# An im2col kernel bound by its DMA engines: eight consecutive channels per partition, and half of the input loaded beside the first stores

## The chip, the cores and the metric

One core of a Trainium2 chip. The metric is the device time of the kernel in microseconds (us), as median of several runs. The profile describes one execution; its span (91.3 us before) is shorter than the timed figure (92.9 us) by 1.6 us.

## The reference

The input is 16 images of 64 channels of 32 x 32 float32 numbers. Each channel gives nine output planes of 30 x 30: the channel shifted by (ki, kj), ki and kj from 0 to 2.

```python
for i in range(h_out):
    for j in range(w_out):
        patch = x[b, :, i:i + kernel_size, j:j + kernel_size].copy()
        cols[b, :, col_idx] = patch.ravel()
        col_idx += 1
```

No arithmetic is done. 1,024 channels of 4,096 bytes come in (4.19 MB), and 1,024 x 9 planes of 3,600 bytes go out (33.18 MB).

## The kernel before

A row is two consecutive channels, and a group is 128 rows, one for each partition. All four groups are loaded at the start. VectorE and ScalarE take turns to copy the nine shifted windows of each channel into an output tile, and SyncE stores the tile. The first group is stored one channel at a time, the others in one piece. There are two output tiles, so the third group waits until the first is stored.

```python
x_v = x.rearrange("b (cp c2) h w -> (b cp) c2 (h w)", c2=CPP)        # CPP = 2
...
for g in range(n_groups):                                            # 4 loads of 1 MB
    nc.sync.dma_start(out=in_tile, in_=x_v[row0 : row0 + P]...)
...
for g in range(n_groups):
    out_tile = out_pool.tile([P, CPP, KK, HO, WO], x.dtype)          # bufs=2
    for c2 in range(CPP):
        for kk in range(KK):
            ...
            if ncopy % 2 == 0:
                nc.scalar.copy(out=dst, in_=src)
            else:
                nc.vector.tensor_copy(out=dst, in_=src)
        if g == 0:
            nc.sync.dma_start(out=out_v[row0 : row0 + P, c2], ...)   # 32,400 bytes per partition
    if g != 0:
        nc.sync.dma_start(out=out_v[row0 : row0 + P]..., ...)        # 64,800 bytes per partition
```

Of the kernel before, what the change touches and what calls it, by code (L numbers as in the profile page):

```python
# [1 line left out]

# [4 lines left out]


def _im2col_fast(ctx, tc, x, K, out, CPP):  # L10
    nc = tc.nc
    P = nc.NUM_PARTITIONS

    B, C, H, W = x.shape
    HO = H - K + 1
    WO = W - K + 1
    KK = K * K

    ROWS = B * C // CPP
    n_groups = ROWS // P  # L20

    x_v = x.rearrange("b (cp c2) h w -> (b cp) c2 (h w)", c2=CPP)
    out_v = out.rearrange("b (cp c2 kk) n -> (b cp) c2 (kk n)", c2=CPP, kk=KK)

    in_pool = ctx.enter_context(tc.tile_pool(name="in_pool", bufs=n_groups))
    out_pool = ctx.enter_context(tc.tile_pool(name="out_pool", bufs=2))

    in_tiles = []
    for g in range(n_groups):
        row0 = g * P  # L30
        in_tile = in_pool.tile([P, CPP, H, W], x.dtype, name="in_tile")
        nc.sync.dma_start(
            out=in_tile,
            in_=x_v[row0 : row0 + P].rearrange("r c2 (h w) -> r c2 h w", h=H),
        )
        in_tiles.append(in_tile)

    for g in range(n_groups):
        row0 = g * P
        in_tile = in_tiles[g]  # L40
        out_tile = out_pool.tile([P, CPP, KK, HO, WO], x.dtype)

        ncopy = 0
        for c2 in range(CPP):
            for kk in range(KK):
                ki, kj = divmod(kk, K)
                src = in_tile[:, c2, ki : ki + HO, kj : kj + WO]
                dst = out_tile[:, c2, kk]
                if ncopy % 2 == 0:
                    nc.scalar.copy(out=dst, in_=src)  # L50
                else:
                    nc.vector.tensor_copy(out=dst, in_=src)  # L52
                ncopy += 1

            if g == 0:
                nc.sync.dma_start(
                    out=out_v[row0 : row0 + P, c2],
                    in_=out_tile[:, c2].rearrange("p kk i j -> p (kk i j)"),
                )

        if g != 0:
            nc.sync.dma_start(
                out=out_v[row0 : row0 + P].rearrange("r c2 n -> r (c2 n)"),
                in_=out_tile.rearrange("p c2 kk i j -> p (c2 kk i j)"),
            )


def _im2col_generic(ctx, tc, x, K, out):
    nc = tc.nc
    P = nc.NUM_PARTITIONS  # L70

    B, C, H, W = x.shape
    HO = H - K + 1
    WO = W - K + 1
    KK = K * K

    x_rows = x.rearrange("b c h w -> (b c) (h w)")
    out_rows = out.rearrange("b ck n -> (b ck) n").rearrange(
        "(bc kk) n -> bc (kk n)", kk=KK
    )  # L80

    n_rows = B * C
    n_groups = (n_rows + P - 1) // P

    in_pool = ctx.enter_context(tc.tile_pool(name="in_pool", bufs=min(n_groups, 4)))
    out_pool = ctx.enter_context(tc.tile_pool(name="out_pool", bufs=2))

    for g in range(n_groups):
        row0 = g * P
        nrows = min(P, n_rows - row0)  # L90

        in_tile = in_pool.tile([P, H, W], x.dtype, name="in_tile_g")
        nc.sync.dma_start(
            out=in_tile[:nrows],
            in_=x_rows[row0 : row0 + nrows].rearrange("r (h w) -> r h w", h=H),
        )

        out_tile = out_pool.tile([P, KK, HO, WO], x.dtype, name="out_tile_g")
        for kk in range(KK):
            ki, kj = divmod(kk, K)  # L100
            src = in_tile[:nrows, ki : ki + HO, kj : kj + WO]
            dst = out_tile[:nrows, kk]
            if kk % 2 == 0:
                nc.scalar.copy(out=dst, in_=src)
            else:
                nc.vector.tensor_copy(out=dst, in_=src)

        nc.sync.dma_start(
            out=out_rows[row0 : row0 + nrows],
            in_=out_tile[:nrows].rearrange("p kk i j -> p (kk i j)"),  # L110
        )


@with_exitstack
def kernel(
    ctx: ExitStack,
    tc: tile.TileContext,
    x: bass.AP,
    kernel_size: bass.AP,
    out: bass.AP,  # L120
):
    nc = tc.nc
    P = nc.NUM_PARTITIONS

    K = int(kernel_size)
    B, C, H, W = x.shape
    HO = H - K + 1
    WO = W - K + 1
    KK = K * K
    assert out.shape == (B, C * K * K, HO * WO)  # L130

    dt_size = mybir.dt.size(x.dtype)

    CPP = 0
    for cand in (2, 1):
        if C % cand:
            continue
        rows = B * C // cand
        if rows % P:
            continue  # L140
        free_bytes = cand * KK * HO * WO * dt_size
        if free_bytes >= 2**16:
            continue
        n_groups = rows // P
        sbuf_need = 2 * free_bytes + n_groups * cand * H * W * dt_size
        if sbuf_need > 190 * 1024:
            continue
        CPP = cand
        break

    if CPP:
        _im2col_fast(ctx, tc, x, K, out, CPP)
    else:
        _im2col_generic(ctx, tc, x, K, out)


# [1 line left out]
_INS = ['x', 'kernel_size']  # L158
_OUTS = [((16, 576, 900), 'float32')]
#: Inputs that are plain numbers.  # L160
_NUMBERS = {'kernel_size': 3}


# [26 lines left out]
```

## Time and profile before

| | before |
|---|---|
| time, median of three runs | 92.85 us (92.7 to 93.08) |
| span of the profile | 91.3 us |
| DMA queue's share of 16 engines' span | 95.7% |
| first load packet starts / last data packet ends | 1.75 / 89.91 us |
| VectorE, ScalarE busy | 22%, 35% |

The trace's packet records: each of the 16 DMA engines moves the data of eight partitions, one packet for each partition and DMA. These records are what the DMA rows of the views sum up, and they are this document's finest measure. They do not name the engine: what is said of single engines comes from fitting the end of one packet to the start of the next. One caution for the views in short windows: a packet is counted whole in the window in which it starts. When packets are long, a share can stand above 1.00, or at 0.00 in the next window, while the engine was simply busy. The windows below are 2 us long and are used only where packets are short.

### The profile page before, as it was taken

Reading aid. Unit: us, or ns where it says so; the run is one execution under the profiler, and the core shown is the slowest. Engines: PE = TensorE matmul, PEld = TensorE weight load, DVE = VectorE, ACT = ScalarE, POOL = GpSimd, SP = SyncE. Lnnn points to the kernel's source line nnn. Section 1 sums busy time; section 2 is a strip of 40 time slices with the busy share of each in tenths; the row PEclk is TensorE's granted clock in tenths of the full one; section 3 lists DMA queues with packets and bytes.
Section 4 is the critical chain, followed back from the end, with each engine's and each line's share of the span. In section 5 each row is a group of like instructions: output and inputs, shape, how many; then the busy total and the mean of one; then the engine's idle time right before and its main releaser. Section 6 shows DMA issues by size and latency. Waiting matters only on the chain.

```text
span 91.3 us, 141 instructions
## 1 busy us (share of the span) xinstructions
DVE 19.6 (22%) x36; ACT 32.0 (35%) x37; POOL 0.2 (0%) x4
## 2 busy tenths in 40 slices
DVE  0059997000000049600000199000000000000000
ACT  5059999991000049980000199920000000000000
POOL 0000000000000000000000000000000000000000
DMA  2899999999999999899999999999999999999960
GB/s 36 373 406 431 427 463 426 412 440 440 426 426 440 554 454 398 369 426 398 454 454 454 454 454 454 454 454 454 454 454 426 426 398 398 426 426 426 426 284 0
DMA packets 1297, 37.37 MB, mean 409 GB/s; under 512 B 145, under 2 KB 145, under 8 KB 145
## 3 DMA queue, kind: packets, MB, share of 16 engines
q1 hardware_dynamic: 1296, 37.37, 95.7%
q14 instruction: 1, 0.00, 0.0%
HBM read 4.19 MB, written 33.18 MB: 409 GB/s over the span
## 4 chain that ended last, share of the span: by engine, by line
DMA 40%; ACT 24%; ACTq 1%; issue 0%
DMA out_dram<-out_tile 34%; ACT out_tile L50 24%; DMA in_tile<-in_x_dram 5%; ACTq L185 1%; ACTq L50 0%
## 5 line engine op out<-in xcount | busy, mean ns | idle before, releaser
L50 ACT COPY out_tile<-in_tile 128x900 f32<-128x900 f32 x36 | 30.7, 938 | 27.2 <-DMA out_dram<-out_tile 23.6
L52 DVE COPY out_tile<-in_tile 128x900 f32<-128x900 f32 x36 | 19.6, 623 | 37.6 <-DMA out_dram<-out_tile 31.9
L50 ACT ACT_TABLE_LOAD x1 | 1.3, 1283 | 0.7 <-PEq L171 0.7
L171 POOL MEMSET const-bfloat16-1.0<- 128x1 bf16 x1 | 0.1, 102 | 0.0
L171 POOL MEMSET const-uint8-127<- 128x1 uint8 x1 | 0.1, 102 | 0.0
L171 POOL MEMSET const-float32-0.0<- 128x1 f32 x1 | 0.1, 99 | 0.2 <-issue 0.2
L171 POOL MEMSET const-float32-1.0<- 128x1 f32 x1 | 0.1, 99 | 0.0
## 6 DMA issues: line engine op xcount, KB each, us to landing
out_dram<-out_tile SPq DMA_DIRECT2D x3, 8100.0 KB, 30.5
out_dram<-out_tile SPq DMA_DIRECT2D x2, 4050.0 KB, 16.6
in_tile<-in_x_dram SPq DMA_DIRECT2D x4, 1024.0 KB, 7.9
```

The costliest lines, as they stand in the source:

```text
L50: nc.scalar.copy(out=dst, in_=src)
L52: nc.vector.tensor_copy(out=dst, in_=src)
L171: nc = _bacc.Bacc("TRN2", target_bir_lowering=False, num_devices=1)
L185: with _tile.TileContext(nc) as tc:
```

## The change

The intent is to start storing earlier. Every partition now owns eight consecutive channels. The input is cut into loads of one, one, two and four channels; the first three are issued at once from ScalarE's queue, and the fourth from the same queue beside the first stores. The first channel is stored in three pieces of three planes. VectorE takes three of five copies instead of every second.

```diff
-    CPP = 0
-    for cand in (2, 1):
...
+    CPP = B * C // P                                   # 8
+    x_v = x.rearrange("b (cp c2) h w -> (b cp) c2 h w", c2=CPP)
+    loads = [(0, 1), (1, 2), (2, CPP // 2), (CPP // 2, CPP)]
...
+    for i in range(len(loads) - 1):
+        load(i, nc.scalar)
+    turn = (0, 1, 0, 1, 0)
+    n = 0
+    for c in range(0, CPP, 2):
+        out_tile = out_pool.tile([P, 2, KK, HO, WO], x.dtype, name="out_tile")
+        for s in range(2):
+            for kk in range(KK):
+                plane(out_tile[:, s], c + s, kk, turn[n % len(turn)])
+                n += 1
+                if c == 0 and s == 0 and kk % K == K - 1:
+                    store(c, 1, kk + 1 - K, kk + 1, out_tile, 0)
+            if c == 0 and s == 1:
+                store(1, 1, 0, KK, out_tile, 1)
+            if c == 0 and s == 0:
+                load(len(loads) - 1, nc.scalar)
+        if c > 0:
+            store(c, 2, 0, KK, out_tile, 0)
```

More of the change, by code (lines that the diff above doesn't have):

```diff
@@ L5 @@
 import concourse.tile as tile
-from concourse import bass_utils, mybir
+from concourse import mybir
 from concourse._compat import with_exitstack
-def _im2col_fast(ctx, tc, x, K, out, CPP):
-    nc = tc.nc
-    P = nc.NUM_PARTITIONS
-    B, C, H, W = x.shape
-    HO = H - K + 1
-    WO = W - K + 1
-    KK = K * K
-    ROWS = B * C // CPP
-    n_groups = ROWS // P
-    x_v = x.rearrange("b (cp c2) h w -> (b cp) c2 (h w)", c2=CPP)
-    out_v = out.rearrange("b (cp c2 kk) n -> (b cp) c2 (kk n)", c2=CPP, kk=KK)
-    in_pool = ctx.enter_context(tc.tile_pool(name="in_pool", bufs=n_groups))
-    out_pool = ctx.enter_context(tc.tile_pool(name="out_pool", bufs=2))
-    in_tiles = []
-    for g in range(n_groups):
-        row0 = g * P
-        in_tile = in_pool.tile([P, CPP, H, W], x.dtype, name="in_tile")
-        nc.sync.dma_start(
-            out=in_tile,
-            in_=x_v[row0 : row0 + P].rearrange("r c2 (h w) -> r c2 h w", h=H),
-        )
-        in_tiles.append(in_tile)
-    for g in range(n_groups):
-        row0 = g * P
-        in_tile = in_tiles[g]
-        out_tile = out_pool.tile([P, CPP, KK, HO, WO], x.dtype)
-        ncopy = 0
-        for c2 in range(CPP):
-            for kk in range(KK):
-                ki, kj = divmod(kk, K)
-                src = in_tile[:, c2, ki : ki + HO, kj : kj + WO]
-                dst = out_tile[:, c2, kk]
-                if ncopy % 2 == 0:
-                    nc.scalar.copy(out=dst, in_=src)
-                else:
-                    nc.vector.tensor_copy(out=dst, in_=src)
-                ncopy += 1
-            if g == 0:
-                nc.sync.dma_start(
-                    out=out_v[row0 : row0 + P, c2],
-                    in_=out_tile[:, c2].rearrange("p kk i j -> p (kk i j)"),
-                )
-        if g != 0:
-            nc.sync.dma_start(
-                out=out_v[row0 : row0 + P].rearrange("r c2 n -> r (c2 n)"),
-                in_=out_tile.rearrange("p c2 kk i j -> p (c2 kk i j)"),
-            )
@@ L68, in _im2col_generic @@
-def _im2col_generic(ctx, tc, x, K, out):
-    nc = tc.nc
-    P = nc.NUM_PARTITIONS
-    B, C, H, W = x.shape
-    HO = H - K + 1
-    WO = W - K + 1
-    KK = K * K
-    x_rows = x.rearrange("b c h w -> (b c) (h w)")
-    out_rows = out.rearrange("b ck n -> (b ck) n").rearrange(
-        "(bc kk) n -> bc (kk n)", kk=KK
-    )
-    n_rows = B * C
-    n_groups = (n_rows + P - 1) // P
-    in_pool = ctx.enter_context(tc.tile_pool(name="in_pool", bufs=min(n_groups, 4)))
-    out_pool = ctx.enter_context(tc.tile_pool(name="out_pool", bufs=2))
-    for g in range(n_groups):
-        row0 = g * P
-        nrows = min(P, n_rows - row0)
-        in_tile = in_pool.tile([P, H, W], x.dtype, name="in_tile_g")
-        nc.sync.dma_start(
-            out=in_tile[:nrows],
-            in_=x_rows[row0 : row0 + nrows].rearrange("r (h w) -> r h w", h=H),
-        )
-        out_tile = out_pool.tile([P, KK, HO, WO], x.dtype, name="out_tile_g")
-        for kk in range(KK):
-            ki, kj = divmod(kk, K)
-            src = in_tile[:nrows, ki : ki + HO, kj : kj + WO]
-            dst = out_tile[:nrows, kk]
-            if kk % 2 == 0:
-                nc.scalar.copy(out=dst, in_=src)
-            else:
-                nc.vector.tensor_copy(out=dst, in_=src)
-        nc.sync.dma_start(
-            out=out_rows[row0 : row0 + nrows],
-            in_=out_tile[:nrows].rearrange("p kk i j -> p (kk i j)"),
-        )
@@ L129 @@
     KK = K * K
-    assert out.shape == (B, C * K * K, HO * WO)
-    dt_size = mybir.dt.size(x.dtype)
-    CPP = 0
-    for cand in (2, 1):
-        if C % cand:
-            continue
-        rows = B * C // cand
-        if rows % P:
-            continue
-        free_bytes = cand * KK * HO * WO * dt_size
-        if free_bytes >= 2**16:
-            continue
-        n_groups = rows // P
-        sbuf_need = 2 * free_bytes + n_groups * cand * H * W * dt_size
-        if sbuf_need > 190 * 1024:
-            continue
-        CPP = cand
-        break
@@ L151 @@
-    if CPP:
-        _im2col_fast(ctx, tc, x, K, out, CPP)
-    else:
-        _im2col_generic(ctx, tc, x, K, out)
+    assert out.shape == (B, C * KK, HO * WO)
+    CPP = B * C // P
+    assert CPP * P == B * C and C % CPP == 0 and CPP % 4 == 0
+    x_v = x.rearrange("b (cp c2) h w -> (b cp) c2 h w", c2=CPP)
+    out_v = out.rearrange("b (cp c2 kk) n -> (b cp) c2 kk n", c2=CPP, kk=KK)
+    in_pool = ctx.enter_context(tc.tile_pool(name="in_pool", bufs=1))
+    out_pool = ctx.enter_context(tc.tile_pool(name="out_pool", bufs=2))
@@ new lines, with load, plane @@
+    loads = [(0, 1), (1, 2), (2, CPP // 2), (CPP // 2, CPP)]
+    home = {}
+    def load(i, queue):
+        c0, c1 = loads[i]
+        t = in_pool.tile([P, c1 - c0, H, W], x.dtype, name=f"in_tile{i}")
+        queue.dma_start(
+            out=t.rearrange("p c h w -> p (c h w)"),
+            in_=x_v[:, c0:c1].rearrange("p c h w -> p (c h w)"),
+        )
+        for c in range(c0, c1):
+            home[c] = (t, c0)
+    def plane(dst, c, kk, engine):
+        t, base = home[c]
+        ki, kj = divmod(kk, K)
+        src = t[:, c - base, ki : ki + HO, kj : kj + WO]
+        if engine == 0:
+            nc.vector.tensor_copy(out=dst[:, kk], in_=src)
+        else:
+            nc.scalar.copy(out=dst[:, kk], in_=src)
@@ new lines, in store @@
+    def store(c, n, k0, k1, t, slot):
+        if n == 1:
+            nc.sync.dma_start(
+                out=out_v[:, c, k0:k1].rearrange("p kk n -> p (kk n)"),
+                in_=t[:, slot, k0:k1].rearrange("p kk i j -> p (kk i j)"),
+            )
+        else:
+            nc.sync.dma_start(
+                out=out_v[:, c : c + n].rearrange("p c kk n -> p (c kk n)"),
+                in_=t.rearrange("p c kk i j -> p (c kk i j)"),
+            )
+    for i in range(len(loads) - 1):
+        load(i, nc.scalar)
```

## The prediction

> **What bounds the kernel now.** I read the busy tenths in 40 slices first, because it says at once which resource has no holes.
>
> ```profile
> DVE  0059997000000049600000199000000000000000
> ACT  5059999991000049980000199920000000000000
> DMA  2899999999999999899999999999999999999960
> ```
>
> VectorE and ScalarE work in three short bursts and are empty more than half of the time; the DMA row is 8 or 9 from the second slice to the last but one. Next the totals and the queues:
>
> ```profile
> DMA packets 1297, 37.37 MB, mean 409 GB/s; under 512 B 145, under 2 KB 145, under 8 KB 145
> ## 3 DMA queue, kind: packets, MB, share of 16 engines
> q1 hardware_dynamic: 1296, 37.37, 95.7%
> ...
> HBM read 4.19 MB, written 33.18 MB: 409 GB/s over the span
> ```
>
> The 16 DMA engines are busy 95.7% of the 91.3 us span. What is left is the two ends. To find them I cut the start into windows of 0.4 us (columns: stretch, length, DVE, ACT, POOL, TensorE clock, DMA share, GB/s):
>
> ```profile
> 0.80:1.20 0.40, 0.00 (x0) 0.40 (x1) 0.00 (x0) 1.00 0.00 0
> 1.20:1.60 0.40, 0.00 (x0) 0.40 (x1) 0.00 (x0) 1.00 0.00 0
> 1.60:2.00 0.40, 0.00 (x0) 0.40 (x1) 0.00 (x0) 1.00 1.19 164
> 2.00:2.40 0.40, 0.00 (x0) 0.01 (x1) 0.00 (x0) 1.00 0.28 41
> 2.40:2.80 0.40, 0.00 (x0) 0.00 (x0) 0.00 (x0) 1.00 0.50 184
> 2.80:3.20 0.40, 0.00 (x0) 0.00 (x0) 0.00 (x0) 1.00 1.01 430
> ```
>
> From 2.8 us on the rate is the full one and stays there. The packet records of the trace, which these views sum up, give the other end: the first load packet starts at 1.64 us, the last data packet ends at 89.79 us, and the sixteen engines finish between 88.72 and 89.79. So 1.6 us lie before the DMA work, 1.5 us behind it, and 88.1 us are DMA work with no hole. Then I asked for the chain of waits in order of time and the timeline, to see whether any copy ever kept the DMA engines waiting:
>
> ```profile
> 5.61 15.29 ACT L50 COPY out_tile<-in_tile 128x900 f32<-128x900 f32 x18 [3.60 <-DMA in_tile<-in_x_dram]
> 5.61 9.77 DVE L52 COPY out_tile<-in_tile 128x900 f32<-128x900 f32 x18 [5.61 <-DMA in_tile<-in_x_dram]
> 9.96 3.72 SPq L56 DMA_DIRECT2D out_dram<-out_tile  x2
> 20.92 39.36 SPq L62 DMA_DIRECT2D out_dram<-out_tile  x3
> 33.09 7.70 ACT L50 COPY out_tile<-in_tile 128x900 f32<-128x900 f32 x9 [12.20 <-DMA out_dram<-out_tile]
> ```
>
> The first store is issued at 9.96 us, while the packets of the four loads run until 13.27 us (first of the stores: 12.20). The later stores are issued at 20.9, about 40.8 and 60.0 us, and by the packet records the work queued ahead of each lasts until some 31, 51 and 70 us. Each store is in the queue some 10 us before its turn, except the first, which has 2.2 us. The chain that ended last names ScalarE for 24% of the span, but that is the way back through the issue of a store that then stood in a queue; it is not time that a faster copy would save.
>
> **What the Trainium skill says.** "DMA: Bandwidth & Descriptors", section "Where 436 GB/s comes from", puts the ceiling of the 16 ports at 435.2 GB/s. The trace agrees: a packet of 64,800 bytes takes 2,394 ns, which is 27.07 bytes per ns and 433 GB/s on 16 engines. The same page, "Issuing engines are not separate DMA queues", says that DMAs from ScalarE and SyncE run on the same 16 engines and interleave, so that a second issuing engine only saves issue time; the kernel before uses one queue, so its trace cannot show it. The same page, "Latency and other measured facts", reports that large power-of-two row pitches in HBM slow copies (207 GB/s per direction at 512 KiB against a full 214, much less at 2 MiB and up); here no run shows it yet. "ScalarE: Activation LUTs", "What ACT_TABLE_LOAD costs", gives 1283 ns for the table load, and that page has it placed right before the first activation; the trace has exactly 1,283 ns, at 0.72 us.
>
> **The change, part by part.**
>
> Bytes: none added or removed. Still 4.19 MB in and 33.18 MB out, with the longest contiguous run of a store unchanged (two channels, 64,800 bytes).
>
> Packets: each DMA engine serves 8 partitions, one packet per partition and DMA. The trace has 309 ns for 8,192 bytes, 1,200 ns for 32,400, 2,394 ns for 64,800. The line through the last two is 0.0369 ns per byte with some 6 ns per packet. Before, one engine does 32 load packets (mean 330 ns with the slow first ones, 10.57 us), 16 of 1,200.8 ns (19.21 us), 24 of 2,394.3 ns (57.46 us), and 9 semaphore writes of 9 ns: 87.32 us. After: loads 8 x (157 + 157 + 309 + 610) ns = 9.86 us plus the same 0.67 us for the slow start, 10.53 us; stores 24 x 405 ns (three planes, 10,800 bytes) = 9.72, 8 x 1,200.8 = 9.61, 24 x 2,394.3 = 57.46; 11 semaphore writes, 0.10. Sum 87.42 us, 0.1 us more than before.
>
> Start of the copies: the first load is now 0.5 MB instead of 1 MB. Before, its packets were done on the last engine at 5.12 us and the copies began at 5.61. Half of the 8 packets' time saved, 8 x 155 ns = 1.24 us, makes this 3.88 and 4.37 us. That is 1.24 us earlier for VectorE and ScalarE, but in a stage in which the DMA engines still have loads to do, so by itself it is worth nothing.
>
> First store: it needs two VectorE and one ScalarE copies. Back to back these step by 9.77/18 = 0.54 us and 15.29/18 = 0.85 us; the last result is there at about 5.5 to 5.6 us, the issue follows within 0.1 us, and a DMA takes some 0.9 us from its issue to its first packet (0.73 to 1.64 at the start). So the first store can flow at 6.6 us. The three early loads (2.1 MB) keep the engines busy until 7.2 to 7.6 us (the second 1 MB load of before ended there). Slack 0.6 us or more, no hole. This is why the split does no harm: the half that was taken from ahead of the stores runs beside them, but it costs the same engine time there.
>
> Afterwards: stores 2 and 3 are issued near 6.6 and 7.9 us, the late load (behind four ScalarE copies) near 7.9. Work in the queues then reaches to 7.4 + 3 x 3.24 + 4.88 = 22 us. Channel 1 is stored from about 10.9 us, the next pair from about 17, when the queues hold work until 31.6. The third pair waits for its buffer until about 32 and needs 6 to 7 us of copies, while work is queued until about 51; the fourth repeats this at 51 and 70. Never closer than 11 us. The new 3:2 split of the copies between VectorE and ScalarE (11 and 7 of 18 in the first pair: 11 x 0.54 = 6.0 and 7 x 0.85 = 5.9 us, against 7.65 us for nine on ScalarE) is a real saving of 1.7 us per pair on a path that has 11 us to spare: worth nothing.
>
> The sum is +0.1 us on 92.85.
>
> **The rivals.**
>
> The loads start late. They now stand in ScalarE's queue. If the table load comes ahead of them there, the first DMA is issued 1.28 us later and all follows: 92.95 + 1.28 = 94.2. For it: in the trace before, the table load runs at 0.72 us, first thing. Against it: it bears the line of the first copy and the skill has it right before that copy, so the three issues (0.8, 0.4, 0.4 us) should precede it, and it then ends at 3.6 us, before the data is there at 4.4. One in five.
>
> Strided HBM. A partition's neighbour is now 32 KiB away on the input and 259,200 bytes on the output (before: contiguous). The input pitch is a power of two, but far below those named; the output pitch is not one. The trace speaks for the port as limit, with HBM having room. If the loads ran at half rate: the early ones would delay everything by up to 5 us, hence 95 to 98. One in twenty.
>
> Loads free beside stores. If reading and writing could go on at once on an engine, the late 2.1 MB (4.9 us) would cost less: 88 to 91. Against it: store packets alone already fill every engine. One in twenty.
>
> A smaller matter is the 1.07 us by which the engines finish apart, which goes back to their uneven start; another start could give or take 0.5 us.
>
> **Range and chances.** The main case has 92.0 to 93.5 (the 0.5 us of the uneven end either way), the late table load 94.2. Predicted 92.9, range 91.9 to 94.3. Two per cent is 1.86 us: faster needs free loads, slower needs strided HBM or a late start plus something else. 5%, 88%, 7%.
>
> **What would show it right or wrong.** Right: DMA row at 9 through the whole span, first packet near 1.6 us, copies from about 4.4 us, first store issued near 5.7 us, no window with a lower DMA share around 7 us, last packet near 90 us; the engines' share near 96%. The table load after the three issues, at about 2.3 us. Wrong: a first packet near 2.9 us (late table load); load packets of 4,096 bytes much above 157 ns or stores of 64,800 above 2,394 ns (stride); a share of the engines clearly below 95% with holes near 7 us (first store too late); or total DMA rate above 435 GB/s between 8 and 22 us (free loads).

## More of the kernel before

All packet times in the document itself count from the first instruction, as the views do. Those in the recorded prediction and expectations were counted from another record: they are 0.12 us too low for the kernel before, and 0.08 us too high for every other run.

The lines that carry the reading of before stand in the prediction. Two more are needed for comparison, the windows of 2 us around the end of the loads (columns: stretch, length, VectorE, ScalarE, GpSimd, TensorE clock, DMA share, GB/s):

```profile
8.00:10.00 2.00, 2.00 (x5) 2.00 (x4) 0.00 (x0) 1.00 0.99 418
10.00:12.00 2.00, 2.00 (x5) 2.00 (x3) 0.00 (x0) 1.00 1.03 406
```

## The result, and the profile after

The changed kernel takes 93.22 us (93.11 to 93.32, four runs) against 92.89 us (92.70 to 93.08) in the same rounds. The ratio is 1.0034, 95% interval 1.0017 to 1.0050. The forecast was 92.9 us, 91.9 to 94.3, "within 2%" at 88%. It held. The change is slower by a third of a per cent, which is small but clear of noise.

The first views to compare are the busy tenths and the queues:

```profile
DVE  0099999100000059800000199400000000000000
ACT  0599999100000059940000199400000000000000
DMA  3899899999889999999999999999999857999990
```

```profile
q1 hardware_dynamic: 1008, 33.18, 84.3%
q10 hardware_dynamic: 576, 4.19, 12.2%
```

The engines' copies moved to the left as intended, and ScalarE's bursts became shorter. The DMA row is as full as it was, and so is the sum of the two queues: 96.5% against 95.7%. The dent near the end (5 and 7) is the counting by start of the 64,800-byte packets; by the packet records the engines are busy there.

The timeline shows the schedule that came out:

```profile
0.73 1.33 ACTq L44 DMA_DIRECT2D in_tile<-in_x_dram  x3
2.10 1.28 ACT L58 ACT_TABLE_LOAD   x1 [2.10 <-issue]
...
4.49 11.92 DVE L56 COPY out_tile<-in_tile 128x900 f32<-128x900 f32 x22 [4.49 <-DMA in_tile<-in_x_dram]
4.50 0.34 ACTq L44 DMA_DIRECT2D in_tile<-in_x_dram  x1
5.34 11.07 ACT L58 COPY out_tile<-in_tile 128x900 f32<-128x900 f32 x13
5.75 5.16 SPq L62 DMA_DIRECT2D out_dram<-out_tile  x4
```

Copies start at 4.49 us and the first store is issued at 5.75 us, 4.2 us earlier than before. Two things differ from the forecast. The late load is issued at 4.50 us, although it stands behind four ScalarE copies in the source. Either the framework moved it forward, as it did in late_sp below, or the sequencer hands copies to its engine and goes on; the trace does not show which. And the first store packet starts only at 9.62 us by the packet records, 3.87 us after the issue. In that time the engines were busy but slow:

```profile
6.00:8.00 2.00, 2.00 (x5) 2.00 (x4) 0.00 (x0) 1.00 1.12 434
8.00:10.00 2.00, 2.00 (x5) 2.00 (x3) 0.00 (x0) 1.00 0.96 314
10.00:12.00 2.00, 2.00 (x4) 2.00 (x3) 0.00 (x0) 1.00 1.00 419
```

The DMA share is 0.96 and only 314 GB/s moved. That is most of the result in one line. It is not a hole: the engines count as busy, but each packet takes longer. From 7.2 to 10.4 us the 16,384-byte packets of the late load take up to 1,032 ns; later, alternating one by one with 10,800-byte store packets, nearly all take 611 ns.

The list of issues (bytes of each, median us from issue to landing) has the same wait in it. A store of 1,350 KB needs 3.2 us of the engines (8 packets of 406 ns each), yet the median of the three lands 13.2 us after its issue:

```profile
out_dram<-out_tile SPq DMA_DIRECT2D x3, 1350.0 KB, 13.2
...
in_tile<-in_x_dram ACTq DMA_DIRECT2D x1, 2048.0 KB, 11.4
```

The sums of packet time for one engine, semaphore writes left out:

| | before | predicted | after |
|---|---|---|---|
| load packets | 10.57 us | 10.53 | 11.14 |
| store packets | 76.68 us | 76.79 | 76.89 |
| sum | 87.25 us | 87.32 | 88.02 |
| engines finish | 88.85 to 89.91 | | 89.57 to 89.86 |

One engine works 0.78 us longer (the mean of the 16), and the mean engine finishes 0.38 us later; the difference is idle time, half of it at the start (0.23 us idle per engine from 1.7 to 2.5 us, against 0.43 before). In these two profiled runs the last packet even ends 0.05 us earlier, because the engines finish within 0.29 us of each other instead of 1.06 us. The timed runs put the difference at 0.33 us.

### The profile page after: what moved, and what is told of

Same layout as the page of the kernel before. It is cut to its first block, busy times and chain, and to the rows that moved or that the text cites. A ratio compares the mean times of both kernels' runs of the same rounds, so it can differ in the third digit from the quotient of the medians.

```text
span 91.3 us, 145 instructions
## 1 busy us (share of the span) xinstructions
DVE 23.4 (26%) x43; ACT 26.1 (29%) x30; POOL 0.2 (0%) x4
## 4 chain that ended last, share of the span: by engine, by line
DMA 43%; DVE 19%; DVEq 1%; issue 0%; SPq 0%
DMA out_dram<-out_tile 39%; DVE out_tile L56 19%; DMA in_tile<-in_x_dram 4%; DVEq L122 1%; DVEq L56 0%; SPq L67 0%
## 5 line engine op out<-in xcount | busy, mean ns | idle before, releaser
L58 ACT COPY out_tile<-in_tile 128x900 f32<-128x900 f32 x29 | 24.8, 939 | 30.0 <-DMA out_dram<-out_tile 28.9
L56 DVE COPY out_tile<-in_tile 128x900 f32<-128x900 f32 x43 | 23.4, 625 | 34.8 <-DMA out_dram<-out_tile 30.3
## 6 DMA issues: line engine op xcount, KB each, us to landing
out_dram<-out_tile SPq DMA_DIRECT2D x3, 1350.0 KB, 13.2
```

Source lines behind the costliest of these rows:

```text
L56: nc.vector.tensor_copy(out=dst[:, kk], in_=src)
L58: nc.scalar.copy(out=dst[:, kk], in_=src)
```

## The experiments

What had to be explained is the time lost in load packets. I measure it in each trace in one way: over all load packets that start after 3.3 us (past the slow start), the time above the usual 159, 309 or 611 ns for 4,096, 8,192 or 16,384 bytes, summed and divided by 16 engines. "Lost" below is this number. It is 0.26 us before and 0.70 us after. Each "lost" is that of one profiled run, and in late_8k, unsplit and pair_first this was the slowest run of its kernel. All runs gave correct results; their timed runs are fast ones except one of w_after. They were sent in three batches, each on another chip, with runs of the kernel before (medians 92.74 to 92.80 us) beside them, so ratios compare better across batches than times do.

### A tiny early store (w_after, w_before)

The first suspicion (theory C) was a slow first write to the output.

```diff
+    warm = in_pool.tile([16, 128], x.dtype, name="warm")
+    nc.vector.memset(warm, 0.0)
+    nc.sync.dma_start(out=out_v[0:16, CPP - 1, 0, 0:128], in_=warm)   # w_before: nc.scalar, the last 16 rows
```

> The changed kernel with one tiny early store (16 partitions x 512 bytes, into a corner of the output that the last store overwrites) from SyncE's queue at some 1 to 2 us. Theory C, the first write to the output is slow and holds up the loads that share the engines: with the first write out of the way, the 16,384-byte load packets fall from a mean of 698 ns to about 615, the first 10,800-byte packet starts near 7 us instead of 9.70, the engines' mean work falls by some 0.7 us, and the last packet ends 0.3 to 0.7 us earlier; time 92.6 to 92.9 against 93.2. Theory S, the late load is slow because of its 32 KiB pitch in HBM or its 16 KiB packets: packets stay near 700 ns and the first store packet near 9.7 us. Theory Q, two queues beside each other cost something at the switch: as S.

> The kernel before with the same tiny early store, from ScalarE's queue while the loads run on SyncE's. Before, 8,192-byte load packets between 11.2 and 13.1 us take up to 646 ns instead of 309, in all some 0.3 us per engine, just ahead of the first store packet. Theory C: this dip is gone, all load packets after 3 us stay near 309 ns; time lower by about 0.3 us (92.6). Theories S and Q: S has no pitch to blame here and Q no second queue, so both leave the dip as it is, or name no cause for it; time 92.9.

w_after took 93.52 us, ratio to before 1.0103 (1.0061 to 1.0146). Its profiled run counts as slow (92.9 us span: one engine finished at 91.36 us, the others by 90.13), so I use only its packets. The tiny store's packets ran at 3.5 to 4.2 us, yet the 16,384-byte packets had a mean of 708 ns, and the first 10,800-byte packet started at 9.65 us. Lost: 0.78 us. w_before took 92.85 us, ratio 1.0009 (0.9997 to 1.0021), lost 0.19 us. Theory C falls: a first write has been done, and the slow phase stays.

### When the late load is issued, and in what pieces (all_first, late_8k, late_4k)

all_first issues all four loads before any copy:

```diff
-    for i in range(len(loads) - 1):
+    for i in range(len(loads)):
         load(i, nc.scalar)
...
-            if c == 0 and s == 0:
-                load(len(loads) - 1, nc.scalar)
```

> The changed kernel with the late load issued right behind the other three, from the same queue, ahead of all copies. Theory C: 16,384-byte packets are slow only from about 1.5 us after the first store's issue (5.75 us) to its first packet; as the load runs from 7.3 us on anyway, the picture is nearly that of the changed kernel: mean near 690 ns. Theory S: mean near 700 ns as well, but slow from the very first packet and independent of the store. Theory Q: the slow packets are those next to the first store packets. Time the same as the changed kernel within 0.3 us (93.2): the moment of the late load is worth nothing in all theories.

93.28 us, ratio 1.0052 (1.0037 to 1.0067). Lost 0.63 us; 16,384-byte packets at a mean of 689 ns, slow from 7.1 us; first store packet at 9.63 us after its issue at 5.65. The moment of the late load is worth nothing, as expected.

late_8k cuts the late load in two, late_4k in four:

```diff
-    loads = [(0, 1), (1, 2), (2, CPP // 2), (CPP // 2, CPP)]
+    loads = [(0, 1), (1, 2), (2, CPP // 2), (CPP // 2, CPP // 2 + 2), (CPP // 2 + 2, CPP)]   # late_4k: (4, 5), (5, 6), (6, 7), (7, 8)
```

> The changed kernel with the late load cut into two of two channels each: 8,192-byte packets, the size that ran at 309 ns in the third load, at the same 32 KiB pitch. Theory S in its form of packet size: packets at 309 to 320 ns, the loss of 0.7 us gone, time 92.6. Theory C: the bytes that pass between 7.3 and 10.5 us are as slow as before (304 to 330 GB/s), the mean of the late 8,192-byte packets is near 345 to 360 ns, time as the changed kernel, 93.2. Theory S in its form of pitch: as C in the mean, but slow packets also before or after that stretch.

> The changed kernel with the late load cut into four of one channel: 4,096-byte packets, a size that ran at 159 ns in the first two loads. Theory P, some 250 ns are lost per load packet between 7.3 us and the first store packet: the rate there falls to 4,096 bytes per 410 ns and engine, 160 GB/s on 16 engines (16 KiB packets had 304 to 330, 8 KiB packets 230 to 240); last packet some 1.7 us later than with 16 KiB packets, time about 95. A theory by which the bandwidth as such is taken away (by descriptors, by copies, by HBM): the rate stays near 230 to 310 GB/s, time 93.5 to 94.3.

late_8k took 94.31 us, ratio 1.0164 (1.0141 to 1.0187), lost 1.32 us. late_4k took 94.22 us, ratio 1.0160 (1.0144 to 1.0176), lost 1.23 us. The same window as above, first late_8k, then late_4k:

```profile
8.00:10.00 2.00, 2.00 (x5) 2.00 (x3) 0.00 (x0) 1.00 1.00 250
```

```profile
8.00:10.00 2.00, 2.00 (x5) 2.00 (x3) 0.00 (x0) 1.00 0.97 211
```

314, 250 and 211 GB/s with pieces of 16, 8 and 4 KiB: both smaller sizes are worse than 16 KiB, in time too, where 8 and 4 KiB are alike. So the large packet is not the culprit. Neither time that I had expected of late_8k (92.6 or 93.2 us) came. My guess of a fixed 250 ns per packet, formed on the first two, predicted 160 GB/s and about 95 us for the third and missed.

### The late load on the other queue (late_sp)

```diff
             if c == 0 and s == 0:
-                load(len(loads) - 1, nc.scalar)
+                load(len(loads) - 1, nc.sync)
```

> The changed kernel with the late load moved to SyncE's queue, behind the third early store in the same queue; nothing is left to cover the time between the third load's end (7.3 to 7.9 us) and the first store packet. Theory L, a store that is issued while loads run needs some 4 us from issue to first packet, whatever lies behind: a hole from about 7.6 to 9.7 us, last packet near 91, time 94.3. Theory P, the first store is only late because the other queue still has packets, and it is these that are slowed (about 250 ns a packet) while the two queues are sorted out: the first store packet starts at 6.7 to 7.9 us, no slow load packets, the loss of 0.7 us gone, time 92.6. Theory S (pitch or size of the 16 KiB reads): the late load's packets are slow wherever they come, mean near 700 ns, time 93.2.

The framework did not build what I had in mind. Nothing in the load depends on the stores, and it was put at the head of SyncE's queue, so it ran beside the other loads from the start:

```profile
0.73 0.37 SPq L44 DMA_DIRECT2D in_tile<-in_x_dram  x1
...
9.59 10.84 DVE L56 COPY out_tile<-in_tile 128x900 f32<-128x900 f32 x20 [9.59 <-DMA in_tile<-in_x_dram]
10.85 5.15 SPq L62 DMA_DIRECT2D out_dram<-out_tile  x4
```

The copies start 5.1 us later than in the changed kernel, and so does the first store. The time is 92.82 us, ratio to before 1.0013 (0.9997 to 1.0028): not slower than the kernel whose copies start at 4.49 us (1.0034, 1.0017 to 1.0050; the intervals overlap). Lost: 0.00 us. The same 16,384-byte packets at the same 32 KiB pitch ran at 611 ns once the start was over, and alternated with packets of another queue. That rules out the pitch, the packet size (theory S) and two queues as such (theory Q). Both queues carried loads there, so a slow phase that needs a store on one queue and loads on the other is not ruled out. Theories L and P were meant for a late load behind the stores, which this run doesn't have; it leaves them open.

### Channel 0 in one store (unsplit)

```diff
-                if c == 0 and s == 0 and kk % K == K - 1:
-                    store(c, 1, kk + 1 - K, kk + 1, out_tile, 0)
+                if c == 0 and s == 0 and kk == KK - 1:
+                    store(c, 1, 0, KK, out_tile, 0)
```

> The changed kernel with channel 0 stored in one piece: the first store is issued at about 7.9 us instead of 5.75. Theories L and P: the slow load packets follow the issue of the first store and begin some 1.5 us after it, at 9.4 instead of 7.3 us; the first three 16,384-byte packets of each engine run at 611 ns, the mean of the late load falls from 698 to 620 to 660 ns; last packet 0.2 to 0.5 us earlier, unless the first store comes after the loads' end (12.5 us) and leaves a hole; time 92.8 to 93.2. Theory S: the first packets of the late load are slow as before, the mean stays near 700 ns.

93.58 us, ratio 1.0110 (1.0076 to 1.0144): worse, not better. The first store was issued at 8.13 us and its first packet came at 12.63 us. The windows show both sides of the first packet's arrival:

```profile
8.00:10.00 2.00, 2.00 (x4) 2.00 (x4) 0.00 (x0) 1.00 1.02 311
10.00:12.00 2.00, 2.00 (x5) 2.00 (x3) 0.00 (x0) 1.00 0.90 279
...
14.00:16.00 2.00, 2.00 (x5) 2.00 (x4) 0.00 (x0) 1.00 1.02 438
```

On nine engines the first two or three 16,384-byte packets ran at 611 ns and the slow ones began at about 9 us, as expected; but then the rate stayed low until the store arrived, and 1.38 us were lost. On five engines the very first packet of the late load, started between 7.5 and 8.2 us, took 1,252 to 1,812 ns, in part before the store was issued. For that I have no explanation. The profiled run is the slowest of the six (94.43 us against a median of 93.58), so part of this may belong to that run alone.

### The owners alone (layout)

```diff
-    x_v = x.rearrange("b (cp c2) h w -> (b cp) c2 (h w)", c2=CPP)
+    x_v = x.rearrange("b (cp g c2) h w -> g (b cp) c2 (h w)", g=n_groups, c2=CPP)
...
-            in_=x_v[row0 : row0 + P].rearrange("r c2 (h w) -> r c2 h w", h=H),
+            in_=x_v[g].rearrange("r c2 (h w) -> r c2 h w", h=H),
```

(The output's view is changed in the same way.)

> The kernel before with nothing changed but the owners: each partition has eight consecutive channels and every load and store takes two of them, so rows lie 32 KiB apart on the input and 259,200 bytes apart on the output. By the prediction ([...]the 16 ports bind): load packets 309 ns, store packets 1,200 and 2,394 ns as before, time 92.8 within 0.3. If the stride costs: packets of one kind above these by the amount that is lost.

92.47 us, ratio 0.9976 (0.9962 to 0.9990). Load packets 309 ns in the median, store packets 1,203 and 2,395 ns in the mean, lost 0.14 us; the time is just under the range that I had given (92.5 to 93.1). The stride costs nothing that these runs can see.

### No store among the loads, and one small store among them (pair_first, one_plane)

These two decide. pair_first issues all loads first and stores the first pair like the others. It is the simplest of all these kernels:

```diff
-    for i in range(len(loads) - 1):
+    for i in range(len(loads)):
         load(i, nc.scalar)
...
-                if c == 0 and s == 0 and kk % K == K - 1:
-                    store(c, 1, kk + 1 - K, kk + 1, out_tile, 0)
-            if c == 0 and s == 1:
-                store(1, 1, 0, KK, out_tile, 1)
-            if c == 0 and s == 0:
-                load(len(loads) - 1, nc.scalar)
-        if c > 0:
-            store(c, 2, 0, KK, out_tile, 0)
+        store(c, 2, 0, KK, out_tile, 0)
```

> The changed kernel with all four loads first and the first pair stored like the others, in one piece, when both channels are copied (at some 10.5 us). Copies run from 4.4 us beside 16,384-byte load packets as in the changed kernel, but no store is issued while many loads are left. If the issue of a store among running loads is what slows them: no slow phase from 7.3 to 10.5 us, 16,384-byte packets at 611 ns (mean below 640), the loads end near 12.6 us, last packet near 89.5, time 92.5 to 92.8 although the first store is issued 4.7 us later than in the changed kernel. If the copies, the packet size or the pitch slow them: slow packets from 7.3 us as before, time 93.2.

92.29 us, ratio 0.9957 (0.9929 to 0.9984), below the 92.5 to 92.8 that I had expected. Its timeline and its windows:

```profile
4.28 11.92 DVE L56 COPY out_tile<-in_tile 128x900 f32<-128x900 f32 x22 [4.28 <-DMA in_tile<-in_x_dram]
10.37 48.30 SPq L67 DMA_DIRECT2D out_dram<-out_tile  x4
```

```profile
8.00:10.00 2.00, 2.00 (x5) 2.00 (x3) 0.00 (x0) 1.00 1.09 467
10.00:12.00 2.00, 2.00 (x5) 2.00 (x4) 0.00 (x0) 1.00 1.03 434
```

The slow phase is gone, with the same loads in the same pieces, and with copies running from 4.28 us. The 16,384-byte packets have a mean of 615 ns; lost 0.09 us. The first store is issued at 10.37 us, 4.6 us later than in the changed kernel, and the kernel is faster by 0.9 us on the medians (by 0.7 us on the ratios to before). It differs from all_first in the stores alone, and there the ratio was 1.0052. (The profiled run is the slowest of the six, 93.02 us: one engine finished at 89.93 us, the others by 88.99. The other five took 92.19 to 92.44.)

one_plane adds to this a store of plane 0 alone, as soon as it is copied:

```diff
+                if c == 0 and s == 0 and kk == 0:
+                    store(c, 1, 0, 1, out_tile, 0)
...
+            nc.sync.dma_start(                                  # the other 17 planes of the first pair
+                out=out_v[:, 0:2].rearrange("p c kk n -> p (c kk n)")[:, HO * WO :],
+                in_=out_tile.rearrange("p c kk i j -> p (c kk i j)")[:, HO * WO :],
+            )
```

> As pair_first, but plane 0 of channel 0 (3,600 bytes per partition, 0.46 MB) is stored alone as soon as it is copied, at some 5.1 us, and the other 17 planes together at some 10.5 us. If the issue of any store among running loads brings on the slow phase: slow packets from about 6.5 us until the 3,600-byte packets come, 3 to 5 us after the issue, then 611 ns again, with a loss of 0.4 to 0.8 us per engine against pair_first; time 93.0 to 93.3. If it takes a large store, or several: no slow packets, time as pair_first.

93.13 us, ratio 1.0050 (1.0015 to 1.0085). The time is as expected, the picture is not. The 3,600-byte packets started from 8.63 us on, 3.5 us after the issue at 5.13, and the load packets in between ran nearly at full rate (0.06 us lost by 10.57 us). The slow phase came with the second, large store, issued at 10.57 us:

```profile
8.00:10.00 2.00, 2.00 (x5) 2.00 (x3) 0.00 (x0) 1.00 0.95 397
10.00:12.00 2.00, 2.00 (x4) 2.00 (x3) 0.00 (x0) 1.00 1.27 446
12.00:14.00 2.00, 2.00 (x5) 2.00 (x4) 0.00 (x0) 1.00 0.76 256
```

By the packet records, with each packet's bytes spread over its time, loads and stores together ran at 290 to 348 GB/s from 11 to 14 us; the first 61,200-byte packet came at 13.99 us. Lost: 0.80 us. In pair_first a store of nearly the same size was issued at nearly the same time and did no harm. The loads still to come do not explain the difference: at that moment 2.8 packets of 16,384 bytes per engine had not started in pair_first, and 3.0 in one_plane. One_plane had 5.7 of its 8 small store packets per engine waiting as well; whether these matter is not shown. In these runs, then, a small store issued among the loads did next to no harm, a large one issued early did, and why the large store of one_plane did and that of pair_first did not is open.

### Slow copies (slow_copies)

```diff
-                plane(out_tile[:, s], c + s, kk, turn[n % len(turn)])
+                plane(out_tile[:, s], c + s, kk, turn[n % len(turn)] if c == 0 else 1)
```

> The changed kernel with all copies of the last three pairs on ScalarE alone: 18 x 0.85 = 15.3 us a pair instead of 6. The prediction says that the copies have 11 us to spare on each pair, so the third is done at 33 + 15.3 = 48.3 us, before its turn at 51, the fourth at 67.5 before 70: time as the changed kernel, 93.2 within 0.3. If the copies are on the path as the chain of waits suggests (19% VectorE), up to 9 us more.

93.56 us, ratio 1.0092 (1.0067 to 1.0117). Here is how the view of the chain misleads. The changed kernel's chain, then that of this run:

```profile
DMA 43%; DVE 19%; DVEq 1%; issue 0%; SPq 0%
```

```profile
ACT 38%; DMA 33%; issue 1%; ACTq 1%
```

By the chain, copies went from 19% to 38% of the span. The copies of a pair did grow from 6 to 15.3 us, and that on three pairs, but the time grew by 0.34 us on the medians (0.6% by the ratios). That is a little over my 0.3. By the packet records the engines have no hole around the last store (issued at 67.7 us); 0.1 us more was lost in load packets than in the changed kernel, and one engine finished at 90.54 us. What made the timed runs slower by more than that is open.

### A version that beats both (best)

The layout kernel with channel 1 copied by VectorE and stored first, so that the first store is issued at 11.00 us, when 3.7 load packets of 8,192 bytes per engine have not started (0.6 when its first packet comes):

```diff
-                if ncopy % 2 == 0:
+                if (ncopy % 2 == 0) if g else (0 < ncopy < KK):      # first group: channel 0 on ScalarE but for its first plane, channel 1 on VectorE
                     nc.scalar.copy(out=dst, in_=src)
...
+            for c2 in (1, 0):                                        # the stores of the first group, after its copies
```

> The kernel before with eight channels per partition (as in layout, 92.47) and the first store later: channel 1 is copied first, by VectorE, and stored at about 10.5 to 11 us, channel 0 by ScalarE and stored at about 12.5 us. The slow load packets of 11.2 to 13.1 us (0.2 to 0.35 us per engine) should go, as only one or two packets per engine are left when the store arrives; last packet near 89.1, time 92.2 to 92.4. If they stay, 92.5; if a hole opens between the last load and the first store, 92.6 or more.

92.33 us (92.28 to 92.52), ratio 0.9953 (0.9934 to 0.9971). Lost: 0.00 us. The windows that answer to those of before:

```profile
8.00:10.00 2.00, 2.00 (x5) 2.00 (x4) 0.00 (x0) 1.00 1.03 434
10.00:12.00 2.00, 2.00 (x5) 2.00 (x3) 0.00 (x0) 1.00 1.02 434
```

All runs beside what they lost:

| kernel | first store issued | its first packet | lost, us | time, us | ratio to before |
|---|---|---|---|---|---|
| pair_first | 10.37 | 11.97 | 0.09 | 92.29 | 0.9957 |
| best | 11.00 | 11.99 | 0.00 | 92.33 | 0.9953 |
| layout | 9.88 | 12.09 | 0.14 | 92.47 | 0.9976 |
| late_sp | 10.85 | 12.27 | 0.00 | 92.82 | 1.0013 |
| before | 9.96 | 12.32 | 0.26 | 92.89 | 1 |
| one_plane | 5.13 | 8.63 | 0.80 | 93.13 | 1.0050 |
| changed | 5.75 | 9.62 | 0.70 | 93.22 | 1.0034 |
| all_first | 5.65 | 9.63 | 0.63 | 93.28 | 1.0052 |
| slow_copies | 5.74 | 9.81 | 0.81 | 93.56 | 1.0092 |
| unsplit | 8.13 | 12.63 | 1.38 | 93.58 | 1.0110 |
| late_4k | 5.65 | 10.18 | 1.23 | 94.22 | 1.0160 |
| late_8k | 5.77 | 10.52 | 1.32 | 94.31 | 1.0164 |

w_after and w_before are left out; they stand in their own section. In the kernels whose first store is issued at or after 9.88 us, when at most 61 KiB of loads per engine have not started, 0.00 to 0.26 us are lost; where a large store is issued with 107 KiB or more to come, 0.63 us and more. One_plane does not fit: its large store was issued with 48 KiB to come, and 0.80 us were lost. One rival is untested: in before, layout and best the first store stands in the queue of the loads, and in all kernels with a large loss it stands in the other queue. No run issues an early large store behind loads in one queue.

## Why the prediction was right or wrong

**The bound was right.** All kernels moved the same bytes but for the tiny extra stores, and no median went below 92.29 us. Long store packets ran at some 433 GB/s in every trace (64,800 bytes in 2,393 to 2,398 ns on 16 engines). The 1.1 us by which copies start earlier (4.49 us measured, 4.37 predicted) were worth nothing, and late_sp shows it the hard way: starting the copies 5.1 us later than in the changed kernel made the kernel no slower.

**The issue times were right, the first store's arrival was wrong.** The table load at 2.10 us after the three issues and the first store's issue at 5.75 us came as forecast. The step that failed is "a DMA takes some 0.9 us from its issue to its first packet (0.73 to 1.64 at the start). So the first store can flow at 6.6 us". The 0.9 us (1.0 us when both times count from the first instruction) were measured on idle engines. With loads running, an early store on the other queue needed 3.5 us (one_plane's small store) to 4.75 us (late_8k), and w_after's tiny one, issued at 1.00 us before any load packet ran, 2.5 us. The trace of before held the warning: its first store was issued at 9.96 us and came at 12.32 us, and from 11.2 us on load packets of 8,192 bytes took up to 646 ns instead of 309 (0.24 us per engine). The prediction gives both store times, and read no hole; it did not ask why the store took so long.

**That no hole opened was luck.** Had the late load been issued near 7.9 us as forecast, and the first store come no sooner than 9.62 us, nothing would have been left to move from 7.8 us, when the third load ended, to some 8.9 us, the late load's first packet (an estimate, with the 1.0 us of the start). The late load was issued at 4.50 us instead and covered this stretch: one error made up for the other. Whether the store would have come sooner with no load behind it, no run shows.

**"It costs the same engine time there" was wrong by 0.7 us.** The prediction put the late load at 8 x 610 ns = 4.88 us per engine; it measured 5.58 us. All other load packets together measured 5.56 us against the predicted 5.65. Shown by pair_first: without an early store among the loads the same packets take 4.92 us. Suggested by one_plane, a single run: a small early store does not do it. Not shown: the mechanism, whether it is the size of a packet or of the whole store that counts, and whether the store has to stand in another queue than the loads.

**The packet sums of the stores were right.** 76.89 us against 76.79 predicted: smaller first stores cost their 0.2 us over before. This term explains the rest of the gap between the changed kernel and pair_first, whose packets take 10.49 us for the loads and 76.64 us for the stores: 0.65 us more in load packets and 0.25 us more in store packets make 0.90 us; the medians differ by 0.93 us, the ratios to before by 0.7 us.

**The uneven end worked in the other direction.** The "smaller matter" of the prediction, 0.5 us either way, hid the loss in the profiled run: the mean engine finished 0.38 us later, the last one 0.05 us earlier. Over the runs the spread varied from 0.3 us to 1.7 us, and it had nothing to do with the change that I could find; it is luck that a single profile contains. So the forecast of 92.9 us came within 0.3 us although one term of its sum was off by 0.7 us, and "within 2%" would have held with a loss more than twice as large; the result does not vouch for these steps.

**The rivals.** The late start did not come: first packet at 1.73 us, and at 1.73 to 1.75 us in before, layout, best and w_before, which have the loads on SyncE. Strided HBM is refuted by layout. Loads free beside stores are refuted: in the changed kernel's records no half microsecond between 8 and 22 us shows more than 431 GB/s for loads and stores together.

**The slack of the later pairs was about right.** The third pair's copies began at 33.03 us (predicted 32) and the fourth's at 52.2 (predicted 51). slow_copies, which used nearly all of the 11 us on each, cost 0.34 us and not nine.

## What to carry to other kernels

When the DMA engines have no hole, an earlier start of copies or stores is worth nothing by itself; add up packets, and ask of a reordering only whether any packet gets slower. In this kernel a large store issued early among the loads slowed them by 0.6 us and more, so it was best to issue all loads first and the first store shortly before they end: 92.3 us, with less code in pair_first. And a latency measured on idle engines (1.0 us) does not hold for a queue beside a busy one (up to 4.75 us).

## What the Trainium skill lacked or had wrong

- "DMA: Bandwidth & Descriptors", "Latency and other measured facts", gives some 600 ns to the first byte of a DMA from SyncE or ScalarE. On idle engines the first packet came 1.0 us after the start of the issuing instruction and 0.63 us after its end (0.73, 1.10 and 1.73 us in the changed kernel), so the figure fits if one counts from the end; the page does not say from where. It has no figure for a store issued early while loads of the other queue are running, where 3.5 to 4.75 us were measured.
- The same page, "Issuing engines are not separate DMA queues", is right that the two queues share the engines. It does not say that load packets can slow down before the first packet of a store comes: those of 16,384 bytes rose from 611 ns to a mean of 806 ns between 7.2 us and the first store packet at 9.62 us in the changed kernel (314 GB/s from 8 to 10 us), and hardly rose beside the small store of one_plane. No page has this.
- The same page, "Queues, rings and completion order", says that an engine drains a packet of typically some 9 to 17 descriptors from one queue before it switches. It has no figure for long rows: in the changed kernel, once store packets had arrived, single rows of 16,384 and 10,800 bytes alternated one by one (in 124 of 128 steps from one packet to the next).
- The slow power-of-two pitches that the same page lists under "Latency and other measured facts" begin at 512 KiB. To this can be added that a 32 KiB pitch on the input and 259,200 bytes on the output cost nothing (layout: 309 ns, 2,395 ns, ratio 0.9976).
